# Four tiles of layer 0's output projection in the gaps of the last recurrent pair, tile 5 of their sum later, and the residual in the memory of keys and values

## The chip, the cores and the metric

The kernel runs on one core of one Trainium2 chip. The metric is the device time of one execution in microseconds (us), as the median of several runs; lower is better. TensorE multiplies matrices, VectorE and ScalarE do the elementwise work, GpSimd and SyncE mostly start transfers. Each engine has its own queue of instructions, in the order that the built program gives, and semaphores order the engines among each other. The profile calls TensorE PE (PEld for its weight loads), VectorE DVE, ScalarE ACT, GpSimd POOL and SyncE SP; SPq and POOLq are the queues of transfers that SP and POOL start.

## The reference

Two layers over 512 frames of width 1024, in float32. Layer 0 (mixer A) is a recurrent mixer of 12 heads of 64 beside a cross-attention of 4 heads into 256 memory tokens; layer 1 (mixer B) is a chunked attention. Both end the same way, and that end is what the change touches:

```python
mix, v_first = rwkv7_time_mix(h, p[..., :3 * D_MIX], ...)   # layer 0
q_mem = p[..., 3 * D_MIX:]
...
mo = memory_attention(q_mem, mem_n, w_mem_kv[layer])
x = x + jnp.concatenate([mix, mo], axis=-1) @ w_out[layer]
x = x + conv_glu(rms_norm(x, ln2[layer]), ffn_in[layer], ...)
```

The concatenation has 1024 columns: 768 of the recurrent heads and 256 of the memory heads. The residual x is added to the projection, and the sum, normed, feeds the gated feed-forward part.

## The kernel before

Activations lie transposed, the 1024 columns in 8 tiles of 128 partitions by 512 frames. Every float32 operand of the large products is split into a high and a low part (`r1h`, `r1l` for activations, `whi`, `wlo` for weights), and a product of a weight tile with an activation tile is three matmuls of 128x128 by 512: high by high (line 198), high by low (line 199), low by high (line 203). `dense` (line 190) writes one output tile: eight k tiles, so 24 matmuls, into one PSUM bank. `mm3` (line 183, matmuls at 184 to 186) is the same for one k tile. `load_w` (178) fetches 512 KB of weights into `wraw` (two buffers) and splits them into `whi`, `wlo` (three each); while `lo_on` is set, ACT writes the negated raw weights into `wlo` (172) and a POOL transfer adds the weights to them (173), else DVE subtracts (175).

The recurrent heads are worked on in six pairs. A pair has three parts: `prepare` (projections; writes the tiles `KB` and `v`, two buffers each), `front` (products inside the chunks of 64 frames; the last to read `KB` and `v`) and `back`. The end of `back` (lines 832 to 870) is a recursion over eight chunks: a small matmul (836), a DVE step (837), the next small matmul, and output matmuls (841) beside it; ACT then copies the result out (845), the heads are normed (`head_rsqrt`: matmuls at 550, a chain of small DVE steps, transposes at 559; then 857 to 859), multiplied by a gate (its product at 184 to 186, line 868), and split into `r1h[i]`, `r1l[i]` (215, 216). So pair 5, the last, gives tile 5, the last of the eight input tiles of the output projection. Memory attention for layer 0 (scores 922, transposes 287, values 297) gives tiles 6 and 7 (882, 883); tiles 0 to 3 come back from DRAM (888), and pair 4 gives tile 4.

`weave` takes generators, each with a cost and a list of what it has done, and emits instructions of the one that is least far in proportion to its cost. A generator may also wait for a condition. The scheduler of the tile framework then orders each engine's queue by readiness and priority. The last weave of layer 0 holds pair 4's `back`, pair 5's `front` and `back`, memory attention, and `ahead`: output tiles 0 and 1 over the seven k tiles other than 5, begun when memory attention and pair 5's recursion have been emitted. PSUM has eight banks: two D (`psd`), four S (`pss`), two L (`psl`). The L banks serve the recursion and the gate product of pairs 0 to 4, and pair 5's gate product; pair 5's recursion uses the D banks; `ahead` puts its two output tiles into the D banks.

After the weave the pools of the recurrent part are closed and `xT`, `r2h`, `r2l` are laid into the memory that comes free; four transfers load the residual into `xT` (line 955). `out_proj` then adds k tile 5 to output tiles 0 and 1, and computes tiles 2 to 7 whole. Each tile is added to `xT` (334), squared and summed (232, 234) and split into `r2h`, `r2l` (239, 240). The feed-forward part follows (its products go to the `psf` banks).

Of the kernel before, what the change touches and what calls it, by code (L numbers as in the profile page):

```python
# [10 lines left out]
F32 = mybir.dt.float32  # L11
# [7 lines left out]
P = 128  # L19
S = 512  # L20
KD = 8
# [60 lines left out]
def weave(gens, tc=None):  # L82

    live = [[g[0], float(g[1]), 0.0, 0.0, g[2] if len(g) > 2 else 0, None] for g in gens]
    now = 0.0
    while live:
        free = [e for e in live if e[5] is None or e[5]()]
        ready = [e for e in free if e[3] <= now]  # L90
        if not ready:
            now = min(e[3] for e in free)
            continue
        e = min(ready, key=lambda x: x[2] / x[1])
        e[5] = None
        try:
            with tc.high_priority(e[4]) if e[4] else ExitStack():
                y = next(e[0])
        except StopIteration:
            live.remove(e)  # L100
            continue
        if callable(y):
            e[5] = y
            continue
        cost, wait = y if isinstance(y, tuple) else (y, 0)
        now += cost
        e[2] += cost
        e[3] = now + wait
# [3 lines left out]
def trunk_kernel(ctx, tc, A, out):  # L112
# [211 lines left out]

    def out_proj(l, act, gain, h_, l_, xT, order, pre=(), done=()):
        for m in range(KD):
            if m < len(pre):
                w, ps = pre[m]
                run(dense(ps[:], [(w, K8)], act, order=[k for k in order if k not in done], start=False))
            else:  # L330
                w = load_w(A["w_out"][l, m])
                ps = ps_d()
                run(dense(ps[:], [(w, K8)], act, order=order))
# [41 lines left out]
    top, bot = slice(0, 64), slice(64, 128)  # L375
    HS = (top, bot)
    actx = ExitStack()
    open_banks(actx, S=4, L=2)
# [64 lines left out]
    def lora_split(idx, raw):  # L443
        w = split_w(raw[:], 1024)
        mraw = flat(kt_("KB", (P, NCH, 3, 64), bufs=2), 1)[:, 0, 0:1024]
        r3 = raw[:].rearrange("p (k f) -> p k f", k=8)
# [94 lines left out]
    def c3(ap):  # L541
        return ap.rearrange("p (c t) -> p c t", c=NCH)
# [23 lines left out]
    def prepare(i, T):  # L566
# [22 lines left out]
        def proj(j, nm, nxt):  # L589
# [7 lines left out]
            V.tensor_tensor(p_[:], ps[:], rho[:], op=ALU.mult)  # L597
            d = kt_("v", bufs=2) if nm == "v" else kt_("krv", bufs=2)
            SC.activation(d[:], p_[:], AF.Copy, scale=om[:, j * 6 + i:j * 6 + i + 1])
            V.scalar_tensor_tensor(d[:, 1:S], p_[:, 0:S - 1], Vc("mu_" + nm, i), d[:, 1:S], op0=ALU.mult, op1=ALU.add)  # L600
# [3 lines left out]
        Ei = kt_("Ei")  # L604
        KB = kt_("KB", (P, NCH, 3, 64), bufs=2)
        AR = kt_("AR", (P, NCH, 2, 64), bufs=2)
# [14 lines left out]
        def keys():  # L621
            k = T["k"]
            SC.activation(kn[:], k[:], AF.Copy, scale=kneg[:, i:i + 1])
            sq = tmp()
# [11 lines left out]
            SC.activation(f[:], th[:], AF.Identity, scale=kah[:, i:i + 1], bias=oka[:, i:i + 1])  # L636
            V.tensor_tensor(kh[:], k[:], f[:], op=ALU.mult)
            V.tensor_tensor(KB[:, :, 0, :], c3(kh[:]), c3(Ei[:]), op=ALU.mult)
# [39 lines left out]
        def bonus():  # L678
            r = T["r"]
            V.tensor_tensor(AR[:, :, 1, :], c3(r[:]), E[:, :, 1:65], op=ALU.mult)  # L680
            rk = tmp()
            V.scalar_tensor_tensor(rk[:], r[:], Vc("r_k", i), kh[:], op0=ALU.mult, op1=ALU.mult)
            rkh, rkl = tmp(F32R), tmp(F32R)
# [17 lines left out]
        yield next(bo)  # L701
        V.tensor_tensor(bon[:], T["pb"][:], T["v"][:], op=ALU.mult)
        T.update(KB=KB, AR=AR, dE=dE, bon=bon, Tt=Tt)
# [3 lines left out]
    def front(i, T):  # L707
        v, KB, AR, Tt = c3(T["v"][:]), T["KB"], T["AR"], T["Tt"]

# [58 lines left out]
    def back(i, T, dst, tiles=own_tiles, go=None):  # L768
# [84 lines left out]
        if go is not None:  # L853
            yield go
        pg = ps_l()
        mm3(pg[:], g2h[:], g2l[:], gsh[:], gsl[:], True, True)
# [59 lines left out]
    qmA = [kt_("kn")[:], kt_("kh")[:]]  # L916
    spare = flat(kt_("KB", (P, NCH, 3, 64), bufs=2), 3)
    ptA = [spare[:, 0], spare[:, 1], spare[:, 2], E[:].rearrange("p c t -> p (c t)")[:, :S]]
    prA = [kt_("a"), kt_("Ei")]
# [8 lines left out]
    def told(g, n):  # L928
        yield from g
        over.add(n)  # L930

    def ahead():
        yield lambda: "mem" in over and "state" in Ts[NPAIR - 1]
        yield from out_ahead(0, act1, AHEAD, 2, pre)

    def later(ns):
        yield 0, ns

    AHEAD = [0, 1, 2, 3, 4, 6, 7]
    a_, b_ = NPAIR - 2, NPAIR - 1  # L940
# [4 lines left out]
            16 * 648 + mem_cost(860)),  # L945
           (ahead(), 14 * 648)], tc)
    lo_on[0] = 0
    actx.close()

    mid = ctx.enter_context(tc.tile_pool(name="mid", bufs=1))  # L950
    xT = mid.tile([P, KD, S], F32, name="xT")
    r2h = mid.tile([P, KD, S], F32R, name="r2h")
    r2l = mid.tile([P, KD, S], F32R, name="r2l")
    for m in range(0, KD, 2):
        nc.sync.dma_start(xT[:, m:m + 2], A["xT"][:, m:m + 2])
    act2 = pair_of(r2h, r2l)
    fctx = ExitStack()
    open_banks(fctx, S=2, F=4)
    open_tmp(fctx, 6)
    out_proj(0, act1, "ln2_0", r2h, r2l, xT, AHEAD + [5], pre, AHEAD)  # L960
    norm_rho(acc, rho[:])
# [319 lines left out]
```

## Time and profile before

| | |
|---|---|
| median of 3 runs | 1376.41 us (1375.87 to 1377.62) |
| span of the profiled execution | 1375.2 us, from its first to its last instruction |
| mean granted TensorE clock | 0.989 of full |
| PE, PEld busy | 1320.1 us (96%), 1073.8 us (78%) |
| DVE, ACT, POOL busy | 827.1 us (60%), 612.6 us (45%), 34.0 us (2%) |
| first matmul of the feed-forward part of layer 0 (`psf`) | at 412.41 us |

The profiled execution's time outside its span isn't recorded with it: the three runs lie 0.7 to 2.4 us above the span, their median 1.2 us. Times in the views are us from the span's start. The view of windows gives the busy time of each engine in a stretch, the granted TensorE clock (1.00 is full speed) and the share of the transfer engines' time. In the chain of waits each row has a start, a duration, and an engine with the tile that it writes and the line; what released it stands in the row above.

### The profile page before, as it was taken

What the parts mean: (1) busy time and instruction counts of PE and PEld (TensorE: products, weight loads), DVE (VectorE), ACT (ScalarE), POOL (GpSimd) and SP (SyncE); (2) the same over time, 40 slices, a digit from 0 to 9 for tenths busy, and PEclk for the clock granted to TensorE, in tenths of its full rate; (3) what the DMA queues carried; (4) which work ended last, traced back from release to release, by engine and by line L of the source; (5) the groups of instructions that cost most, each with busy time, mean ns of one, the idle gap of its engine ahead of it and who ended that gap; (6) DMA issues with size and microseconds to landing.
All of it is one profiled execution on the core that took longest, in us unless ns stands there. A gap on an engine that the chain in (4) does not pass through costs nothing.

```text
span 1375.2 us, 20877 instructions
## 1 busy us (share of the span) xinstructions
PE 1320.1 (96%) x8266; PEld 1073.8 (78%) x8266; DVE 827.1 (60%) x1752; ACT 612.6 (45%) x1022; POOL 34.0 (2%) x55
## 2 busy tenths in 40 slices
PE   6989999999799999999999999999999999999996
PEld 4877777777588888888888878786788888888886
DVE  7876788878356655655333667657665565563324
ACT  6556565555234333333222566657443333332321
POOL 3000000000000000000000000000000000000000
PEclk9999999999899999999999999999999999999998
DMA  5366544462132233233232422222223223223332
GB/s 181 112 181 135 107 104 111 104 135 50 52 117 92 92 100 100 92 97 99 84 98 85 157 87 85 82 94 94 92 92 107 92 93 103 96 88 86 106 91 75
DMA packets 63507, 139.18 MB, mean 101 GB/s; under 512 B 24625, under 2 KB 28337, under 8 KB 63409
## 3 DMA queue, kind: packets, MB, share of 16 engines
q1 hardware_dynamic: 60672, 127.89, 29.8%
q0 software_dynamic: 2736, 9.96, 4.2%
q8 instruction: 65, 1.06, 0.3%
q14 instruction: 34, 0.27, 0.1%
HBM read 131.01 MB, written 6.82 MB: 100 GB/s over the span
## 4 chain that ended last, share of the span: by engine, by line
PE 78%; DVE 12%; ACT 4%; DMA 3%; issue 2%; SPq 0%; DVEq 0%; ACTq 0%; POOLq 0%
PE psf L198 12%; PE psf L199 12%; PE psf L203 12%; PE psd L198 10%; PE psd L199 10%; PE psd L203 10%; DVE Xu L667 2%; DVE Xs L669 1%; PE pss L1098 1%; DVE Xs L662 1%; DVE ML L720 1%; DVE wlo L175 1%; PE psd L1048 1%; PE pss L297 1%; ACT whi L169 1%
## 5 line engine op out<-in xcount | busy, mean ns | idle before, releaser
L175 DVE TENSOR_TENSOR wlo<-wraw,whi 128x1024 fp32r<-128x1024 f32 x183 | 219.0, 1197 | 132.3 <-PE psd L203 118.2
L169 ACT CAST whi<-wraw 128x1024 fp32r<-128x1024 f32 (+1 forms) x202 | 207.8, 1030 | 163.9 <-DMA wraw<-in_ffn_out_dram 41.5
L198 PE MATMUL psd<-r1h,whi 128*128 128x512 f32 x336 | 137.6, 410 | 7.5 <-ACT r1h L215 3.8
L198 PE MATMUL psf<-r2h,whi 128*128 128x512 f32 x352 | 137.1, 390 | 0.0
L198 PE MATMUL psf<-r1h,whi 128*128 128x512 f32 x352 | 137.1, 390 | 0.0
L199 PE MATMUL psf<-r1l,whi 128*128 128x512 f32 x352 | 136.9, 389 | 0.0
L199 PE MATMUL psf<-r2l,whi 128*128 128x512 f32 x352 | 136.9, 389 | 0.0
L199 PE MATMUL psd<-r1l,whi 128*128 128x512 f32 x336 | 134.9, 401 | 0.2 <-DVE r1l L216 0.2
L203 PE MATMUL psd<-r1h,wlo 128*128 128x512 f32 x336 | 91.3, 403 | 3.9 <-DMA wlo<-in_wA_dram 3.9
L199 PE MATMUL psd<-f3l,whi 128*128 128x512 f32 (+1 forms) x238 | 88.6, 377 | 0.0
L198 PE MATMUL psd<-f3h,whi 128*128 128x512 f32 (+1 forms) x238 | 88.5, 376 | 0.0
L359 DVE TENSOR_TENSOR tmp<-psf,rho 128x512 f32<-128x512 f32 x44 | 30.4, 692 | 94.7 <-PE psf L203 94.7
L203 PE MATMUL psf<-r1h,wlo 128*128 128x512 f32 x352 | 86.9, 389 | 0.0
L203 PE MATMUL psf<-r2h,wlo 128*128 128x512 f32 x352 | 86.9, 389 | 0.0
L198 PEld LDWEIGHTS psd<-r1h,whi 128*128 128x128 f32 x336 | 65.0, 193 | 23.7 <-ACT r1h L215 4.0
L198 PE MATMUL psd<-r2h,whi 128*128 128x512 f32 (+1 forms) x200 | 77.0, 389 | 0.8 <-ACT r2h L1105 0.7
L199 PE MATMUL psd<-r2l,whi 128*128 128x512 f32 (+1 forms) x200 | 76.4, 385 | 0.7 <-DVE r2l L216 0.7
L198 PEld LDWEIGHTS psf<-r2h,whi 128*128 128x128 f32 x352 | 66.1, 188 | 13.7
L199 PEld LDWEIGHTS psf<-r1l,whi 128*128 128x128 f32 x352 | 66.1, 188 | 13.7
L203 PEld LDWEIGHTS psf<-r1h,wlo 128*128 128x128 f32 x352 | 66.1, 188 | 13.7
L203 PEld LDWEIGHTS psf<-r2h,wlo 128*128 128x128 f32 x352 | 66.1, 188 | 13.7
L199 PEld LDWEIGHTS psf<-r2l,whi 128*128 128x128 f32 x352 | 66.1, 188 | 13.6
(352 smaller groups left out, 2420.9 us busy)
## 6 DMA issues: line engine op xcount, KB each, us to landing
wraw<-in_ffn_in_dram SPq DMA_DIRECT2D x88, 512.0 KB, 3.3
wraw<-in_ffn_out_dram SPq DMA_DIRECT2D x32, 448.0 KB, 3.3
wraw<-in_wA_dram SPq DMA_DIRECT2D x20, 512.0 KB, 3.9
wlo<-in_wA_dram POOLq DMA_DIRECT2D x17, 512.0 KB, 8.0
wraw<-in_w_out_dram SPq DMA_DIRECT2D x16, 512.0 KB, 3.4
wraw<-in_ffn_out_dram SPq DMA_DIRECT2D x16, 512.0 KB, 4.2
wraw<-in_wB_dram SPq DMA_DIRECT2D x8, 512.0 KB, 3.4
Lr<-d SPq DMA_DIRECT2D x24, 128.0 KB, 6.3
```

Source lines behind the costliest of these rows:

```text
L169: SC.copy(hi[:, :n], raw)
L175: V.tensor_tensor(lo[:, :n], raw, hi[:, :n], op=ALU.subtract)
L198: PE.matmul(ps, wh[:, j * P:(j + 1) * P], ah, start=start and n == 0, stop=False)
L199: PE.matmul(ps, wh[:, j * P:(j + 1) * P], al, start=False, stop=False)
L203: PE.matmul(ps, wl[:, j * P:(j + 1) * P], act(k)[0], start=False, stop=stop and n == len(ks) - 1)
L297: PE.matmul(pso[hs, :], vm[l][:, kt, (f * 2 + hh) * 64:(f * 2 + hh + 1) * 64], pts[f, hh, kt], start=kt == 0, stop=kt == 1)
L359: V.tensor_tensor(v[:], pv[:], rho[:], op=ALU.mult)
L662: V.scalar_tensor_tensor(X[:, m, q + 1:], L1[:, :, 0], X[:, m, q:q + 1], X[:, m, q + 1:], op0=ALU.mult, op1=ALU.add)
L667: V.tensor_tensor(uv, L1.rearrange("p i o -> p o i").to_broadcast([P, k, n]), X[:, 0:k, q:q + 1].to_broadcast([P, k, n]), op=ALU.mult)
L669: V.tensor_tensor(X[:, 0:k, q + 1:], X[:, 0:k, q + 1:], uv, op=ALU.add)
L720: V.tensor_tensor(ML[:, h, c4 * 4:c4 * 4 + 4, 0:128], ps[h][:], C("m1").unsqueeze(1).to_broadcast([P, 4, 128]), op=ALU.mult)
L1048: PE.matmul(pt, r1h[:, k, ts], wh[:, ws], start=k == 0, stop=False)
```

## The change

Layer 0 alone is touched. Six things are done together.

- `xT` gets memory of its own from the start, and the two buffers of `KB` and of `v` become parts of it (`KBs`, `vs`), as do three of the four tiles for memory attention's transposed weights (`ptA`) and the scratch of the low-rank weights. What is freed elsewhere equals what `xT` takes.
- `ahead` begins when memory attention and pair 4's `back` have been emitted, not when pair 5's recursion has; its first two tiles go to the L banks, two more follow in the D banks once the recursion is emitted. Pair 5's gate product moves from an L bank to an S bank for that.
- `ahead` has cost 0, and the new key of `weave` lets such a generator go on only when no other is ready.
- Its k order is 0, 1, 2, 3, 6, 7, 4, so that pair 4's tile comes last.
- The rows of the four weight tiles that belong to k tile 5 come in one transfer of 256 KB (line 951 of the changed kernel) and are split once, into the memory of `a` and `Ei`; so no weight tile is held for the end. When pair 5 is done, twelve matmuls (`mm3`) and four adds close output tiles 2, 3, 0, 1.
- The residual is loaded inside `ahead` (line 953 of the changed kernel), and `out_proj` only norms the first four tiles and computes tiles 4 to 7.

```diff
 def weave(gens, tc=None):
...
-        e = min(ready, key=lambda x: x[2] / x[1])
+        e = min(ready, key=lambda x: (x[1] <= 0, x[2] / (x[1] or 1.0)))
...
-    def out_proj(l, act, gain, h_, l_, xT, order, pre=(), done=()):
+    def out_proj(l, act, gain, h_, l_, xT, order, pre=(), done=(), added=0):
         for m in range(KD):
+            if m < added:
+                norm_tile(xT[:, m], m, gain, h_, l_)
+                continue
             if m < len(pre):
...
     HS = (top, bot)
+    mid = ctx.enter_context(tc.tile_pool(name="mid", bufs=1))
+    xT = mid.tile([P, KD, S], F32, name="xT")
+    KBs = [xT[:, 3 * u:3 * u + 3].rearrange("p m s -> p (m s)").rearrange("p (c a t) -> p c a t", c=NCH, a=3)
+           for u in range(2)]
+    vs = [xT[:, 6], xT[:, 7]]
...
-            d = kt_("v", bufs=2) if nm == "v" else kt_("krv", bufs=2)
+            d = vs[i % 2] if nm == "v" else kt_("krv", bufs=2)[:]
...
-        KB = kt_("KB", (P, NCH, 3, 64), bufs=2)
+        KB = KBs[i % 2]
...
-        pg = ps_l()
+        pg = ps_s() if i == NPAIR - 1 else ps_l()
...
-    spare = flat(kt_("KB", (P, NCH, 3, 64), bufs=2), 3)
-    ptA = [spare[:, 0], spare[:, 1], spare[:, 2], E[:].rearrange("p c t -> p (c t)")[:, :S]]
+    ptA = [xT[:, 0], xT[:, 1], xT[:, 2], E[:].rearrange("p c t -> p (c t)")[:, :S]]
...
+    AHEAD = [0, 1, 2, 3, 6, 7, 4]
+    NA = 4
+    w5 = {}
+
     def ahead():
-        yield lambda: "mem" in over and "state" in Ts[NPAIR - 1]
-        yield from out_ahead(0, act1, AHEAD, 2, pre)
+        yield lambda: "mem" in over and "back" in over
+        raw = tmp(F32, (P, NA, P))
+        for m in range(NA):
+            if m == 2:
+                yield lambda: "state" in Ts[NPAIR - 1]
+            w = load_w(A["w_out"][0, m])
+            if m == 0:
+                nc.sync.dma_start(raw[:], A["w_out"][0, 0:NA, :, 5 * P:6 * P].rearrange("m p f -> p m f"))
+                for u in range(0, KD, 2):
+                    nc.sync.dma_start(xT[:, u:u + 2], A["xT"][:, u:u + 2])
+            ps = (ps_l if m < 2 else ps_d)()
+            pre.append(ps)
+            yield from dense(ps[:], [(w, K8)], act1, order=AHEAD, stop=False)
+            if m == 0:
+                w5["h"], w5["l"] = (kt_(n_, (P, NA, P), dt=F32R) for n_ in ("a", "Ei"))
+                split_to(w5["h"][:], w5["l"][:], raw[:])
...
-    AHEAD = [0, 1, 2, 3, 4, 6, 7]
...
-           (ahead(), 14 * 648)], tc)
+           (ahead(), 0)], tc)
+    for m in (2, 3, 0, 1):
+        mm3(pre[m][:], w5["h"][:, m], w5["l"][:, m], r1h[:, 5], r1l[:, 5], False, True)
+        V.tensor_tensor(xT[:, m], xT[:, m], pre[m][:], op=ALU.add)
     lo_on[0] = 0
     actx.close()
 
-    mid = ctx.enter_context(tc.tile_pool(name="mid", bufs=1))
-    xT = mid.tile([P, KD, S], F32, name="xT")
+    mid = ctx.enter_context(tc.tile_pool(name="mid2", bufs=1))
     r2h = mid.tile([P, KD, S], F32R, name="r2h")
     r2l = mid.tile([P, KD, S], F32R, name="r2l")
-    for m in range(0, KD, 2):
-        nc.sync.dma_start(xT[:, m:m + 2], A["xT"][:, m:m + 2])
...
-    out_proj(0, act1, "ln2_0", r2h, r2l, xT, AHEAD + [5], pre, AHEAD)
+    out_proj(0, act1, "ln2_0", r2h, r2l, xT, AHEAD + [5], added=NA)
```

The remaining lines of the diff drop a `[:]` where a tile has become a view, and point the low-rank scratch at `xT`.

Lines in the changed kernel are 3 to 24 higher: 550, 559, 836, 841, 845, 882, 883 are now 558, 567, 844, 849, 853, 890, 891. On PE the two programs read alike, waits included, up to the gate product of pair 4. Three places differ in what the prediction speaks of.

On PE, the last two steps of pair 5's recursion, behind memory attention, before (`psd_4509` and `psd_4510` are the recursion's banks, `psd_4596` is output tile 0):

```order
L841 MATMUL psd_4510<-Lr_4352,AR_4351 64x64 x2
L836 MATMUL psd_4509<-AR_4351,Lr_4352 64x64 x2
L841 MATMUL psd_4510<-Lr_4352,AR_4351 64x64 x4
L198 MATMUL psd_4596<-r1h_68,whi_4591 128x512
L199 MATMUL psd_4596<-r1l_69,whi_4591 128x512
```

And now (`psd_4498` and `psd_4499` are the recursion's banks, `psl_4570` is output tile 0, `psl_4624` output tile 1):

```order
L198 MATMUL psl_4570<-r1h_68,whi_4560 128x512
L199 MATMUL psl_4570<-r1l_69,whi_4560 128x512
L203 MATMUL psl_4570<-r1h_68,wlo_4561 128x512 x4
L844 MATMUL psd_4498<-AR_4340,Lr_4341 64x64 x2
L849 MATMUL psd_4499<-Lr_4341,AR_4340 64x64 x2
L203 MATMUL psl_4570<-r1h_68,wlo_4561 128x512 x3
L849 MATMUL psd_4499<-Lr_4341,AR_4340 64x64 x2
L198 MATMUL psl_4624<-r1h_68,whi_4619 128x512
```

Six matmuls of output tile 0 stand before the recursion's last step and three before its last output matmuls; two and five more stand, in the same way, before the two steps ahead of these rows, and another five of tile 0 earlier, beside memory attention, where three matmuls of pair 5's gate product have moved away.

On PE, the end of the work ahead, before (`pss_4632` and `pss_4668` are the norm of pair 5's heads, `psd_4625` output tile 1, `psd_4729` output tile 2):

```order
L203 MATMUL psd_4625<-r1h_68,wlo_4621 128x512 x7
L559 MATMUL pss_4668<-cst_66,tmp_4666 128x128 x4
L198 MATMUL psd_4596<-r1h_68,whi_4591 128x512
L199 MATMUL psd_4596<-r1l_69,whi_4591 128x512
L203 MATMUL psd_4596<-r1h_68,wlo_4592 128x512
L198 MATMUL psd_4625<-r1h_68,whi_4620 128x512
L199 MATMUL psd_4625<-r1l_69,whi_4620 128x512
L203 MATMUL psd_4625<-r1h_68,wlo_4621 128x512
L198 MATMUL psd_4729<-r1h_68,whi_4725 128x512
```

And now (`psd_4718` is output tile 3; `a_4613` and `Ei_4614` hold the rows of k tile 5; `psd_4799` is output tile 4):

```order
L203 MATMUL psd_4718<-r1h_68,wlo_4714 128x512 x7
L184 MATMUL psd_4672<-r1h_68,a_4613 128x512
L185 MATMUL psd_4672<-r1l_69,a_4613 128x512
L186 MATMUL psd_4672<-r1h_68,Ei_4614 128x512
L184 MATMUL psd_4718<-r1h_68,a_4613 128x512
L185 MATMUL psd_4718<-r1l_69,a_4613 128x512
L186 MATMUL psd_4718<-r1h_68,Ei_4614 128x512
L184 MATMUL psl_4570<-r1h_68,a_4613 128x512
L185 MATMUL psl_4570<-r1l_69,a_4613 128x512
L186 MATMUL psl_4570<-r1h_68,Ei_4614 128x512
```

Where six matmuls of k tile 5 followed the norm directly, twelve now follow some thirty-six matmuls of output tiles 2 and 3, which stand behind the norm's transposes.

On ACT, around the end of memory attention, before (`E_91` is the last transposed weight tile, `psd_4510` the recursion's result):

```order
L290 COPY E_91<-pss_4550 128x512
L882 CAST r1h_68<-pss_4556 128x512
L845 COPY tmp_4585<-psd_4510 128x512
L848 ACTIVATE tmp_4587<-tmp_4585 128x512
L858 ACTIVATE tmp_4585<-tmp_4585,vec_67 128x512
L215 CAST r1h_68<-tmp_4585 128x512
L169 CAST whi_4762<-wraw_4760 128x1024
```

And now:

```order
L290 COPY xT_76<-pss_4528 128x512
L215 CAST a_4613<-tmp_4557 128x512
L290 COPY E_95<-pss_4539 128x512
L890 CAST r1h_68<-pss_4545 128x512
L169 CAST whi_4713<-wraw_4711 128x1024
L172 ACTIVATE wlo_4714<-wraw_4711 128x1024
L853 COPY tmp_4609<-psd_4499 128x512
L856 ACTIVATE tmp_4611<-tmp_4609 128x512
L169 CAST whi_4795<-wraw_4793 128x1024
```

The cast of k tile 5's rows (`a_4613`) stands ahead of the attention's last copy, and the two steps of output tile 3's weights (`whi_4713`, `wlo_4714`) stand ahead of the copy of the recursion's result.

More of the change, by code (lines that the diff above doesn't have):

```diff
@@ L444, in lora_split @@
         w = split_w(raw[:], 1024)
-        mraw = flat(kt_("KB", (P, NCH, 3, 64), bufs=2), 1)[:, 0, 0:1024]
+        mraw = xT[:, 3 * idx:3 * idx + 2].rearrange("p m s -> p (m s)")
         r3 = raw[:].rearrange("p (k f) -> p k f", k=8)
@@ L597, in proj @@
             V.tensor_tensor(p_[:], ps[:], rho[:], op=ALU.mult)
-            d = kt_("v", bufs=2) if nm == "v" else kt_("krv", bufs=2)
-            SC.activation(d[:], p_[:], AF.Copy, scale=om[:, j * 6 + i:j * 6 + i + 1])
+            d = vs[i % 2] if nm == "v" else kt_("krv", bufs=2)[:]
+            SC.activation(d, p_[:], AF.Copy, scale=om[:, j * 6 + i:j * 6 + i + 1])
             V.scalar_tensor_tensor(d[:, 1:S], p_[:, 0:S - 1], Vc("mu_" + nm, i), d[:, 1:S], op0=ALU.mult, op1=ALU.add)
@@ L622, in keys @@
             k = T["k"]
-            SC.activation(kn[:], k[:], AF.Copy, scale=kneg[:, i:i + 1])
+            SC.activation(kn[:], k, AF.Copy, scale=kneg[:, i:i + 1])
             sq = tmp()
@@ L636, in keys @@
             SC.activation(f[:], th[:], AF.Identity, scale=kah[:, i:i + 1], bias=oka[:, i:i + 1])
-            V.tensor_tensor(kh[:], k[:], f[:], op=ALU.mult)
+            V.tensor_tensor(kh[:], k, f[:], op=ALU.mult)
             V.tensor_tensor(KB[:, :, 0, :], c3(kh[:]), c3(Ei[:]), op=ALU.mult)
@@ L679, in bonus @@
             r = T["r"]
-            V.tensor_tensor(AR[:, :, 1, :], c3(r[:]), E[:, :, 1:65], op=ALU.mult)
+            V.tensor_tensor(AR[:, :, 1, :], c3(r), E[:, :, 1:65], op=ALU.mult)
             rk = tmp()
-            V.scalar_tensor_tensor(rk[:], r[:], Vc("r_k", i), kh[:], op0=ALU.mult, op1=ALU.mult)
+            V.scalar_tensor_tensor(rk[:], r, Vc("r_k", i), kh[:], op0=ALU.mult, op1=ALU.mult)
             rkh, rkl = tmp(F32R), tmp(F32R)
@@ L701, in prepare @@
         yield next(bo)
-        V.tensor_tensor(bon[:], T["pb"][:], T["v"][:], op=ALU.mult)
+        V.tensor_tensor(bon[:], T["pb"][:], T["v"], op=ALU.mult)
         T.update(KB=KB, AR=AR, dE=dE, bon=bon, Tt=Tt)
@@ L707, in front @@
     def front(i, T):
-        v, KB, AR, Tt = c3(T["v"][:]), T["KB"], T["AR"], T["Tt"]
+        v, KB, AR, Tt = c3(T["v"]), T["KB"], T["AR"], T["Tt"]
         ML = kt_("ML", (P, 2, NCH, 192), bufs=2)
```

## Prediction

> **What bounds the kernel now.** I read the page first.
>
> ```profile
> span 1375.2 us, 20877 instructions
> ...
> PE 1320.1 (96%) x8266; PEld 1073.8 (78%) x8266; DVE 827.1 (60%) x1752; ACT 612.6 (45%) x1022; POOL 34.0 (2%) x55
> ...
> PE   6989999999799999999999999999999999999996
> ...
> PEclk9999999999899999999999999999999999999998
> ```
>
> PE bounds the kernel. A slice is 34.4 us; the eleventh (344 to 378) has a 7 for PE and an 8 for the clock, and from the twelfth on PE reads 9 up to the last slice but one. So I take what is saved before 412 us, where the feed-forward part begins, as saved at the end: all that follows hangs on PE and moves with it. The changed stretch is the bad slice. The windows view, cut where the clock or the load changes, shows it:
>
> ```profile
> 351.60:355.00 3.40, 2.05 (x34) 1.45 (x31) 1.74 (x5) 0.61 (x2) 0.00 (x0) 1.00 0.00 0
> 355.10:358.40 3.30, 3.30 (x10) 2.52 (x9) 0.00 (x0) 0.87 (x2) 0.00 (x0) 0.50 0.00 0
> ...
> 367.50:371.20 3.70, 0.00 (x0) 0.00 (x0) 2.07 (x3) 1.43 (x2) 0.00 (x0) 1.00 0.00 0
> 372.20:376.80 4.60, 2.09 (x5) 1.07 (x4) 3.04 (x4) 2.09 (x2) 0.00 (x0) 0.50 0.83 289
> 376.90:382.40 5.50, 5.50 (x13) 4.34 (x14) 2.52 (x4) 2.36 (x4) 0.00 (x0) 0.50 0.89 329
> 382.60:412.40 29.80, 29.80 (x133) 24.65 (x132) 15.45 (x20) 12.55 (x16) 0.00 (x0) 1.00 0.27 89
> ```
>
> The first columns are the stretch, its length and PE's busy time; the third from the end is the granted clock. PE is part idle to 355, at half clock to 358.4, idle from 367.5 to 371.2, and half idle and then busy at half clock to 382.4. The chain of waits names the causes:
>
> ```profile
> 351.38 0.59 ACT r1h L882
> ...
> 353.66 0.36 PE psd L836 x4
> 354.04 0.29 DVE AR L837
> 354.38 0.33 PE psd L841 x4
> 354.71 0.43 PE psd L198
> ...
> 362.64 0.79 PE pss L550 x8
> ...
> 367.00 0.45 PE pss L559 x4
> ...
> 371.96 3.42 DMA xT<-in_xT_dram
> 375.46 0.67 issue
> 376.13 0.69 DVE xT L334
> 376.86 0.80 PE psd L198
> ...
> 405.15 1.81 PE psd L203 x8
> ...
> 410.59 1.81 PE psd L203 x8
> 412.41 0.23 PE psf L198
> ```
>
> To 354.71 the recursion's steps alternate between PE (836) and DVE (837); the norm of pair 5's heads (550, 559) ends in tile 5 at 371.96; then the residual's load, which could only start when the recurrent pools were free, holds the first add, and with it the bank of output tile 2, until 376.86. From there it is matmuls: an output tile takes 410.59 - 405.15 = 5.44 us, so one matmul 5.44 / 24 = 0.227 us at full clock.
>
> **The sum.** The projection has 8 x 24 = 192 matmuls, 43.5 us at full clock. With the norm's two groups (0.79 and 0.45) that is 44.8 us, and it takes 412.41 - 354.71 = 57.7. The 12.9 us over are the half clock and the two empty stretches. The matmuls stay the same in number (eight k tiles for eight tiles); what changes is where they stand.
>
> *Start of the recursion's last steps.* Five matmuls of output tile 0 are added beside memory attention and three of the gate product leave. The windows view shows no idle PE there:
>
> ```profile
> 333.36:344.00 10.64, 10.64 (x180) 9.04 (x181) 7.53 (x27) 7.56 (x23) 0.00 (x0) 1.00 0.01 4
> ```
>
> So two more cost 2 x 0.227 = 0.45 us; bounds 0 (all in small gaps that the busy time hides) and 5 x 0.227 = 1.1.
>
> *Recursion.* From the attention's last values (351.38, where ACT copies them out) to 354.71 are 3.3 us. They hold three steps of the recursion and its last output matmuls, four PE pieces of 0.33 to 0.36, 1.4 in all, so PE is idle for 1.9. Put in are 2 + 5 + 6 + 3 = 16 matmuls, 3.6 us: 1.9 fill the gaps, 1.7 push the recursion's end. Bounds 0 and 3.6. Its end moves to 354.71 + 0.45 + 1.7 = 356.9.
>
> *After it.* 192 - 21 = 171 matmuls are left, 38.8 us, plus 1.24 for the norm and 0.68 for the gate product: 40.7 us of PE work, if it never stops. I go through what it could stop for.
> - The norm's first group stands 12 matmuls (2.7 us) behind the recursion. It needs the copy and the square on ACT, which now queue behind the second step of tile 3's weights: that needs the buffer which tile 0's last matmul frees, 0.3 us before the recursion's end, and takes about 1.05 us (the cast of equal size below). With two more ACT steps of 0.6 the group is ready about 2.1 us after the recursion's end: covered by 0.6.
> - From the end of that group (363.43) to the transposes (367.00) are 3.57 us of small DVE steps. 15 matmuls, 3.4 us, stand between: 0.2 us lost.
> - From the transposes to the end of tile 5 are 371.96 - 367.00 = 5.0 us, plus up to 1.05 for a weight cast put ahead of the high part on ACT. Tiles 2 and 3 put 36 matmuls, 8.2 us, and the gate product in between: covered by 3 us. This is the 3.7 us empty stretch, gone.
> - The residual: two loads now go out before the pair's front has ended, two when the attention's values are read, near 352, and take 3.42; the first add is due near 374. The load that held 371.96 to 376.86 is gone with 19 us of cover.
> - Output tile 3's low weights are put on POOL's queue near 358. The view of transfers has, in its last column, the us from issue to landing:
>
> ```profile
> wraw<-in_w_out_dram SPq DMA_DIRECT2D x16, 512.0 KB, 3.4
> ...
> wlo<-in_w_out_dram POOLq DMA_DIRECT2D x2, 512.0 KB, 7.9
> ```
>
>   So they land near 366; they are first used 29 matmuls (6.6 us), the gate product and the transposes themselves behind the 364 of the row above, near 371.7.
> - The adds and norms of the first four tiles came one per output tile; now they come together beside tile 4. The groups of 376.8 to 412.4, with the mean ns of one behind the first bar:
>
> ```profile
> L169 ACT CAST whi<-wraw 128x1024 fp32r<-128x1024 f32 x6 | 6.3, 1052 | 12.7 <-issue 8.5 <-PE psd L199 4.1
> L175 DVE TENSOR_TENSOR wlo<-wraw,whi 128x1024 fp32r<-128x1024 f32 x5 | 6.1, 1220 | 0.0
> ...
> L334 DVE TENSOR_TENSOR xT<-xT,psd 128x512 f32<-128x512 f32 x7 | 4.7, 685 | 14.5 <-PE psd L203 14.5
> ```
>
>   Tile 4 needs only the first add's bank, which is closed three matmuls into the twelve: one split (1.22, whose buffer tile 3 frees) and one add (0.69) beside 12 matmuls of 2.7 us. Covered by 0.8. The weights of tiles 4 to 6 are split before that, those of tile 7 have over 10 us.
>
> SP's queue is reordered too: two residual loads and tile 4's weights stand ahead of the writes that carry pair 5's triangular inverse through DRAM. The timeline of SP, and of the engines that wait:
>
> ```profile
> 324.95 1.82 SPq L675 DMA_DIRECT2D Tt<-d  x4
> ...
> 329.07 0.43 SPq L772 DMA_DIRECT2D tmp<-in_g_dram  x1
> ```
>
> ```profile
> 330.42 0.89 DVE L776 STREAM_TRANSPOSE AR<-Tt 32x256 f32<-32x256 f32 x2
> ...
> 336.16 0.69 PE L781 MATMUL pss<-AR,ML 32*32 32x32 f32 x32
> ...
> 349.48 0.58 ACT L290 COPY E<-pss 128x512 f32<-128x512 f32 x1 [0.33 <-PE pss L287]
> ```
>
> The inverse (`Tt`) is taken up by DVE at 330.42 and its result by PE only at 336.16. Even if the queue or the shared transfer engines hold it by as much as a load of 512 KB takes (3.4), that stays inside the 5.7 us between the two. I take 0; bounds 0 and, if nothing hid it, 3.4.
>
> Sum: the feed-forward part starts at 356.9 + 40.7 + 0.2 = 397.8 in place of 412.41, 14.6 us sooner. Span 1375.2 - 14.6 = 1360.6; the median lay 1.2 above the span, so **1361.8 us**.
>
> The clock carries part of it: it read 0.50 in rows of 3.3, and of 4.6 and 5.5 us, and 1.00 elsewhere. The Trainium skill ("TensorE: Matmul & The Clock Gate", Part 1: The HAM clock gate) says the clock is halved after an idle window of about 3.4 us and given back after a busy one, the windows running free. In this case's rows the half clock from 355.10 followed a stretch in which PE was busy for 2.05 of 3.40 us, so a thin window was enough. By the Trainium skill's idle window the filled recursion stays warm and the time is 1361.8; the trace agrees with the length (3.3 us at 0.50), not with the idleness. By the row a window that is merely thin may cost the first rival below.
>
> **Rivals.**
> 1. *The clock still drops.* If the window over the recursion again counts as quiet, about 3.4 us after it run at half clock and do half the work: 1.7 us lost, 1363.5; twice, 1365.2. Against it: sixteen matmuls bring that stretch from 2.05 to nearly 3.4 busy. For it: the steps of the recursion are small matmuls, and a window's phase can shift. 14%.
> 2. *PE is fed too late.* The covers of 0.6 and 0.8 us are thin. If tile 4 waited for all four adds and a further split, 4 x 0.69 + 1.22 = 4.0 us, and the norm's first group for one more ACT step, about 1, it would be 5 us: 1366.8; half of it 1364.3. For: DVE and ACT do in one burst what was spread; against: they are half idle there (15.45 and 12.55 of 29.80). 10%.
> 3. *Slower: the transfer of k tile 5's rows stops two engines.* Its cast stands on ACT ahead of the attention's last copy, and its split on DVE between two steps of the recursion. It is the only transfer of its kind, in short pieces, and follows the 329.07 row on SP. Its turn on ACT comes where the last copy stood, 349.48, 20 us later. Every us beyond is lost whole, and slower than before begins at 349.5 + 14.6 = 364.1, 35 us after issue. The rows above give 3.4 to 7.9, so a landing after 40 us, 5 beyond that point, which gives 1376.4 + 5 = 1381, has 2%.
> 4. *It doesn't do what it says.* If keys, values and residual in one tile made pair i + 1 wait for pair i's reads, five stages would lose more than the gaps give, or all of it. But queues and waits read alike in both programs up to the gate product of pair 4. Then 1376; 2%.
>
> **Chances.** The forecast has 72%, rivals 14, 10, 2 and 2. Its own bounds: the recursion's push of 0 to 3.6 for 1.7, the start's of 0 to 1.1 for 0.45, put it between 1359.6 and 1364.3; the inverse's 3.4, which I hold for hidden, would reach 1365.2 from the forecast. The range reaches into the first two rivals, 1359.5 to 1366. A measurement of this kernel can tell about 0.2%, 2.8 us: faster by more 96%, within 2% (rival 4), slower 2% (rival 3).
>
> **What would show it.** After the change the first `psf` matmul stands near 398. The recursion's last output matmuls (line 849) end near 357, and matmuls to `psl` stand between its steps with no idle row for PE from 352 to 398 of over 0.5 us. The clock reads 1.00 in every window there. The adds at line 973 wait for PE and not for a transfer. Wrong would be: a clock row of 0.50 behind 355; a PE wait for the add of line 973 or for `wlo`; ACT waiting for `tmp<-in_w_out_dram` before 350; or a first 330 us that differ by more than 0.5 us.

## The result and the profile after

| | before | after |
|---|---|---|
| median of four runs each, on one chip | 1377.01 us (1375.87 to 1378.16) | 1368.09 us (1365.91 to 1371.56) |
| ratio | 1 | 0.9933 (95% interval 0.9913 to 0.9953) |
| median of all runs in the comparisons below | 1378.1 us (40 runs, 1374.3 to 1383.6) | 1366.9 us (17 runs, 1362.8 to 1371.6) |
| span of the profiled execution, granted clock | 1375.2 us, 0.989 | 1364.8 us, 0.993 |

The change is faster by 0.67% in the first comparison, 8.9 us; over all runs it is 11.1 us. The later comparisons ran on other chips, with medians of before from 1377.1 to 1379.8; in the two with six runs of the change it was 12.2 and 10.9 us faster. The forecast was 14.6 us less, 1361.8, with a range up to 1366.0: the sign and most of the mechanism held, the size did not.

The page of the changed kernel, the rows that answer to those of before:

```profile
span 1364.8 us, 20881 instructions
...
PE 1316.1 (96%) x8266; PEld 1070.6 (78%) x8266; DVE 825.4 (60%) x1751; ACT 615.1 (45%) x1025; POOL 35.5 (3%) x57
...
PE   6989999999999999999999999999999999999996
...
PEclk9999999999999999999999999999999999999998
```

The 7 and the 8 of the eleventh slice are gone. The windows view, cut at the gate product of pair 4, at the end of memory attention's values, at the recursion's end and at the first feed-forward matmul:

```profile
95.90:102.70 6.80, 5.52 (x24) 4.16 (x25) 2.41 (x9) 1.64 (x3) 0.86 (x1) 0.50 1.06 263
...
334.90:353.90 19.00, 18.69 (x293) 14.65 (x292) 11.08 (x34) 11.20 (x29) 0.00 (x0) 1.00 0.01 3
353.90:360.20 6.30, 6.30 (x54) 4.17 (x53) 1.83 (x5) 1.86 (x3) 0.00 (x0) 1.00 0.47 166
360.20:401.20 41.00, 41.00 (x186) 33.98 (x187) 24.73 (x42) 18.93 (x26) 0.86 (x1) 1.00 0.36 103
```

PE is busy throughout from 353.9 to 401.2, all of it at clock 1.00: none of the three holes of before is left. But the feed-forward part starts at 401.2, not at 397.8. Part of that is ahead of the change: the gate product of pair 4 stands at 334.9 in this execution and at 333.0 in the one before, although both programs are the same up to there, and the first row shows 6.8 us at half clock where before had 3.4. (A first 330 us that differ by more than 0.5 us was one of the prediction's signs of being wrong; experiment 1 looks into it.) The rest is the stretch from 353.9 to 360.2: 6.3 us, in place of 3.4. Here it is in the timeline of PE, row by row:

```profile
353.87 0.33 PE L844 MATMUL psd<-AR,Lr 64*64 64x64 f32 x4
354.04 0.28 PE L849 MATMUL psd<-Lr,AR 64*64 64x64 f32 x4
354.25 0.50 PE L199 MATMUL psl<-r1l,whi 128*128 128x512 f32 x1
354.59 0.40 PE L198 MATMUL psl<-r1h,whi 128*128 128x512 f32 x1
354.91 0.33 PE L844 MATMUL psd<-AR,Lr 64*64 64x64 f32 x4
355.08 0.28 PE L849 MATMUL psd<-Lr,AR 64*64 64x64 f32 x4
355.29 0.50 PE L199 MATMUL psl<-r1l,whi 128*128 128x512 f32 x1
355.63 0.39 PE L198 MATMUL psl<-r1h,whi 128*128 128x512 f32 x1
355.86 0.39 PE L199 MATMUL psl<-r1l,whi 128*128 128x512 f32 x1
...
356.63 0.33 PE L844 MATMUL psd<-AR,Lr 64*64 64x64 f32 x4
356.79 0.28 PE L849 MATMUL psd<-Lr,AR 64*64 64x64 f32 x4
357.00 0.50 PE L198 MATMUL psl<-r1h,whi 128*128 128x512 f32 x1
...
358.60 0.33 PE L844 MATMUL psd<-AR,Lr 64*64 64x64 f32 x4
358.76 0.28 PE L849 MATMUL psd<-Lr,AR 64*64 64x64 f32 x4
358.98 0.96 PE L203 MATMUL psl<-r1h,wlo 128*128 128x512 f32 x3
359.87 0.33 PE L849 MATMUL psd<-Lr,AR 64*64 64x64 f32 x4
```

Read the starts. Inside a group one projection matmul follows the other by 0.23 us (355.63, 355.86). The first of a group holds the next one off by 0.34 (354.25 to 354.59), and the last one holds the recursion's small matmul off by 0.32 (354.59 to 354.91): each switch there and back costs 0.20 us beside the matmuls. The four groups take 0.66, 1.34, 1.60 and 0.89 us, 4.49 in all, where 16 matmuls at 0.227 are 3.63. And the gaps that they fill, in the timeline of PE before, are these:

```profile
351.96 0.33 PE L836 MATMUL psd<-AR,Lr 64*64 64x64 f32 x4 [0.27 <-DVE AR L837]
...
352.94 0.33 PE L836 MATMUL psd<-AR,Lr 64*64 64x64 f32 x4 [0.53 <-DVE AR L837]
...
353.66 0.33 PE L836 MATMUL psd<-AR,Lr 64*64 64x64 f32 x4 [0.27 <-DVE AR L837]
...
354.38 0.33 PE L841 MATMUL psd<-Lr,AR 64*64 64x64 f32 x4 [0.27 <-DVE AR L837]
```

1.34 us, not 1.9. (The windows view of before says the same: 3.40 us with PE busy for 2.05 leave 1.35.) So most of what the 16 matmuls take is pushed onto the recursion's end. What was to be found out: is that the price of the groups, what are they worth then, and is the early 1.9 us the change's or the execution's?

### The profile page after: what moved, and what is told of

Same layout as the page of the kernel before. It is cut to its first block, busy times and chain, and to the rows that moved or that the text cites. A ratio compares the mean times of both kernels' runs of the same rounds, so it can differ in the third digit from the quotient of the medians.

```text
span 1364.8 us, 20881 instructions
## 1 busy us (share of the span) xinstructions
PE 1316.1 (96%) x8266; PEld 1070.6 (78%) x8266; DVE 825.4 (60%) x1751; ACT 615.1 (45%) x1025; POOL 35.5 (3%) x57
## 4 chain that ended last, share of the span: by engine, by line
PE 78%; DVE 12%; ACT 4%; DMA 3%; issue 2%; SPq 1%; DVEq 0%; ACTq 0%; POOLq 0%
PE psf L198 12%; PE psf L199 12%; PE psf L203 12%; PE psd L198 10%; PE psd L199 10%; PE psd L203 10%; DVE Xu L675 2%; DVE Xs L677 1%; PE pss L1122 1%; PE psl L203 1%; DVE Xs L670 1%; DVE ML L728 1%; PE pss L297 1%; PE psd L1072 1%; PE pss L1108 1%
## 5 line engine op out<-in xcount | busy, mean ns | idle before, releaser
L175 DVE TENSOR_TENSOR wlo<-wraw,whi 128x1024 fp32r<-128x1024 f32 (+1 forms) x181 | 216.5, 1196 | 132.5 <-PE psd L203 118.2
L198 PE MATMUL psd<-r1h,whi 128*128 128x512 f32 x318 | 127.4, 401 | 1.2 <-ACT whi L169 1.2
L199 PE MATMUL psd<-r1l,whi 128*128 128x512 f32 x318 | 124.9, 393 | 0.0
L203 PE MATMUL psd<-r1h,wlo 128*128 128x512 f32 x318 | 86.7, 405 | 4.4 <-DMA wlo<-in_wA_dram 4.4
L198 PEld LDWEIGHTS psf<-r2h,whi 128*128 128x128 f32 x352 | 66.1, 188 | 13.6
L198 PEld LDWEIGHTS psf<-r1h,whi 128*128 128x128 f32 x352 | 66.1, 188 | 13.6
```

Of the source, the lines that this page charges most:

```text
L175: V.tensor_tensor(lo[:, :n], raw, hi[:, :n], op=ALU.subtract)
L198: PE.matmul(ps, wh[:, j * P:(j + 1) * P], ah, start=start and n == 0, stop=False)
L199: PE.matmul(ps, wh[:, j * P:(j + 1) * P], al, start=False, stop=False)
L203: PE.matmul(ps, wl[:, j * P:(j + 1) * P], act(k)[0], start=False, stop=stop and n == len(ks) - 1)
```

## Experiments

The table holds one profiled execution a row, read at the same four places, in us; half clock is the length of the 0.50 rows. "Pushed" is from the end of memory attention's values to the recursion's end.

| kernel | gate product at | half clock between 90 us and it | gate product to first psf | pushed | recursion's end to psf | half clock in there |
|---|---|---|---|---|---|---|
| before | 333.0 | 3.4 | 79.2 | 3.4 | 57.5 | 3.4 + 10.2 |
| before, again | 332.7 | 3.4 | 78.8 | 3.5 | 57.0 | 3.4 + 10.2 |
| change | 334.9 | 6.8 | 66.3 | 6.3 | 41.0 | none |
| change, second | 334.7 | 6.8 | 66.3 | 6.3 | 41.0 | none |
| change, third | 336.4 | 3.4 + 6.8 | 68.9 | 6.3 | 41.0 | 6.8, at 340.6 |
| change, fourth | 331.2 | 3.4 | 66.3 | 6.3 | 41.0 | none |
| empty recursion | 331.9 | 3.4 | 70.3 | 3.4 | 49.0 | 6.8, at 353.8 |
| residual alone | 333.3 | 6.8 | 74.5 | 3.4 | 52.8 | 3.4 + 3.4 |
| fewer in gaps | 334.3 | 6.8 | 66.7 | 4.9 | 42.8 | none |
| projection rated | 336.9 | 3.4 + 3.4 + 3.4 | 72.1 | - | 38.2 | 6.8, at 340.8; 3.4, at 371.5 |
| two tiles | 334.6 | 6.8 | 66.5 | 5.8 | 40.9 | none |

**1. Is the early shift the change's?** The changed kernel, unedited, three more times, and the kernel before once more. The first:

> The changed kernel once more, nothing edited. Theory: its program is the same as before up to 318 us, and the 1.9 us by which its profile was late at the gate product (334.98 for 333.02) are one more half-clock window and slower transfers of that one execution. Then this profile has the gate product anywhere from 332.5 to 335.5, the half-clock windows ahead of 330 us differ in number or place between the profiles, and the spans of the timed runs follow the lost clock: 1.37 us for each 0.001 of granted clock. Rival: the shared memory makes the first 330 us slower; then the gate product stands at 334.5 or later again with the same windows. Time 1365.5 to 1371.5 either way, 8 to 9 us below before.

Measured: 1366.05 us (six runs, 1362.79 to 1369.25), ratio 0.9908 (0.9888 to 0.9928); the gate product at 334.7, again with 6.8 us of half clock near 96. This alone did not tell the two apart. The kernel before:

> The kernel before once more, nothing edited, for a second profile of it. Theory: the gate product of pair 4 moves by up to 2 us from 333.02, with the windows of half clock ahead of it; the windows behind 350 us come back (355 and 372 to 382), since the empty stretches there are part of the program. Rival: 333.0 within 0.3, and the shift of 1.9 us then belongs to the change. Time 1376 to 1378.5.

Measured: 1376.29 us, the gate product at 332.7, 3.4 us of half clock near 98; the windows over the recursion and behind the norm came back at their places (353.9 and 371.0). The change a third time:

> The changed kernel a third time, for its clock windows and the gate product's place. Theory: the gate product lies between 331.9 and 335 according to whether the half-clock window near 96 to 102 lasted 3.4 or 6.8 us; from the gate product to the first feed-forward matmul 66.3 us whatever happened ahead. Rival (the change itself delays the first 330 us): 334.8 again with a window of 3.4.

Measured: 1370.47 us, and the gate product later still, with three half-clock rows behind 90 us where there had been one:

```profile
98.20:101.60 3.40, 3.40 (x20) 2.45 (x19) 0.00 (x0) 0.00 (x0) 0.00 (x0) 0.51 1.05 261
169.90:176.70 6.80, 6.80 (x73) 5.25 (x73) 4.06 (x8) 3.22 (x6) 0.00 (x0) 0.50 0.15 48
340.60:347.40 6.80, 6.80 (x80) 5.39 (x78) 2.79 (x14) 3.27 (x12) 0.00 (x0) 0.50 0.01 2
```

The third of them lies inside the stretch counted on: it costs 2.6 us there (68.9 for 66.3). The forecast of 66.3 whatever happened ahead was wrong by that. The fourth time:

> The changed kernel a fourth time, beside the two-tile version, for more times and one more profile. Theory: median 1366 to 1370, 9 to 12 us below before; from the gate product to the first feed-forward matmul 66.3 us, or 1.7 us more for each 3.4 us of half clock inside it; the gate product at 333 or 334.8 or 336.4 according to the half-clock windows near 96 and 170. Rival (the early shift belongs to the change): never below 334.5.

Measured: 1366.18 us (six runs), ratio 0.9922 (0.9900 to 0.9945). In its profiled execution:

```profile
96.70:100.10 3.40, 3.40 (x21) 2.43 (x19) 0.00 (x0) 0.23 (x1) 0.00 (x0) 0.50 1.05 279
331.20:350.30 19.10, 18.79 (x294) 14.73 (x295) 11.08 (x34) 11.22 (x30) 0.00 (x0) 1.00 0.02 5
350.30:356.50 6.20, 6.20 (x53) 4.05 (x53) 1.83 (x5) 1.82 (x3) 0.00 (x0) 1.00 0.50 166
356.50:397.50 41.00, 41.00 (x188) 34.00 (x187) 24.72 (x42) 18.96 (x26) 0.86 (x1) 1.00 0.34 103
```

The gate product stands at 331.2, ahead of both profiles of before. The rival that the change delays the first 330 us falls. Taking off half of the half clock ahead of it, the gate product lies at 331.3 and 331.0 before, and at 331.5, 331.3, 331.3 and 329.5 in the change; the last is the only one of the six with no half clock near 23 us either, where the others had 3.4 or 6.8. So the shift goes with the execution's own clock windows and not with the program. Whether the change makes such windows more frequent, two profiles of before can't tell; the granted clocks of the timed runs (mean 0.992 in 17 runs of the change, 0.988 in 36 of before) give no sign of it: their difference is worth some 11.5 us of half clock, and the rows that went behind the recursion had 13.6. The windows also go with part of the spread of the timed runs: the change's two fastest (1362.8 and 1362.9) were granted 0.995 and 0.996 of the clock, its slowest three (1369.6, 1370.5 and 1371.6) 0.991, 0.989 and 0.989. Another part does not show in the granted clock, and its cause is open: at 0.989 runs of before took from 1374.6 to 1380.1. A comparison of one execution with one can therefore be off by several us here.

**2. What are the matmuls between the recursion's steps worth?** They were taken out:

```diff
             if m == 0:
...
+                w1 = load_w(A["w_out"][0, 1])
+                yield lambda: "state" in Ts[NPAIR - 1]
             ps = (ps_l if m < 2 else ps_d)()
             pre.append(ps)
+            if m < 2:
+                SC.copy(ps[:, 0:2], Ts[NPAIR - 1]["yc"][:, 0:2])
```

The copy writes two columns of the bank from the recursion's output, so that its first matmul can't come sooner. The weights of tile 1 and the split of k tile 5's rows are asked for ahead of it. The five matmuls of tile 0 beside memory attention move behind the recursion too.

> The change, but its first two output tiles start only when the recursion's output has been copied, so that no projection matmul stands between the recursion's steps. Theory now: a group of projection matmuls between two steps costs some 0.2 us beside its matmuls (the first row after a switch stands 0.33 before the next one, not 0.23), so the 16 matmuls in four groups hid only 0.8 us; the stretch from the attention's last values to the recursion's end goes back from 6.3 to 3.5 us, the matmuls stand behind it, and the time is 0.8 us above the change with the clock at 1.00, or 2.5 us above it where the thin stretch halves the clock for one window of 3.4 us. The forecast's own account (1.9 us of gaps filled): 1.9 us above the change, 3.6 with the window. Rival, that the groups cost more than the gaps give: at or below the change.

Measured: 1370.52 us (ratio 0.9944, 0.9924 to 0.9965), 4.5 above the change on the same chip. Its windows over the recursion and behind it:

```profile
349.90:353.30 3.40, 2.09 (x38) 1.48 (x37) 1.73 (x5) 0.59 (x1) 0.00 (x0) 1.00 0.85 292
353.80:360.60 6.80, 6.80 (x20) 5.57 (x19) 0.00 (x0) 0.89 (x4) 0.00 (x0) 0.50 0.00 1
360.60:402.20 41.60, 41.60 (x187) 34.39 (x186) 24.72 (x42) 19.10 (x25) 0.86 (x1) 1.00 0.34 102
```

The recursion is back at 3.4 us, PE 2.09 of 3.40 busy, and 6.8 us of half clock follow. From the gate product to psf it takes 70.3 for 66.3: 4.0, of which 6.8 / 2 = 3.4 are the clock (PE is busy for all 6.8) and the remaining 0.6 what all 21 matmuls had hidden. The price of 0.8 for gaps alone held roughly; one window was expected and two came. The forecast's 1.9 us of filled gaps would have given 1.9 + 3.4 = 5.3. The rival that groups cost more than they give fell.

**3. Does every further matmul in there cost its full time?**

```diff
+                yield lambda: "state" in Ts[NPAIR - 1]
             ps = (ps_l if m < 2 else ps_d)()
```

The rest is as in experiment 2. Without its copy the scheduler still puts ten matmuls into the gaps.

> The change with the first tile's matmuls asked for only behind the recursion, so that they take second place: 10 matmuls instead of 16 stand between its steps, in groups of 2, 4, 2 and 2. Theory (0.2 us a group beside its matmuls, 1.34 us of gaps): from the attention's last values to the recursion's end 3.4 + 10 x 0.227 + 4 x 0.2 - 1.34 = 5.1 us, where the change took 6.3; the six matmuls stand behind it, the clock stays at 1.00, and the time is that of the change within 1 us. Rival (no cost of a switch): 4.3 us, and the time 0 to 1 us below the change. Rival (the clock needs all sixteen): a half-clock row over the recursion and 1.7 to 3.4 us above the change.

Measured: pushed 4.9 us, nearer the 5.1 of the theory than the 4.3 without a cost of switching; 1368.68 us (ratio 0.9922, 0.9897 to 0.9948), as the change. From ten to sixteen matmuls the push grows by 1.4 us, 0.23 for each: with four groups of these sizes the gaps are full, and no more is hidden. The two-tile version of experiment 6 lies between, with 14 matmuls and 5.8 us.

```profile
353.30:358.20 4.90, 4.90 (x48) 3.02 (x47) 1.83 (x5) 1.04 (x2) 0.00 (x0) 1.00 0.62 214
358.20:401.00 42.80, 42.55 (x194) 35.04 (x193) 24.77 (x42) 19.76 (x27) 0.86 (x1) 1.00 0.33 99
```

Ten matmuls also kept the clock at 1.00, in the one profile taken.

**4. Must the projection be confined to gaps?**

```diff
-           (ahead(), 0)], tc)
+           (ahead(), 28 * 648)], tc)
```

> The change with one number: the projection's share in the weave is its own cost and no longer 0, so that it isn't confined to gaps. Tiles 0 and 1 then stand whole ahead of the recursion's last three steps. Theory: those steps run through an empty PE again (1.1 us of gaps, and one or two half-clock windows, 1.7 or 3.4 us), and only tiles 2 and 3, 9.5 us of matmuls, are left to cover the 12 to 17 us from the recursion's end to tile 5, so 2 to 6 us more are lost: 5 to 10 us above the change. Rival: the order among the steps does not matter as long as PE has work; within 1 us of the change.

Measured: 1369.92 us, ratio 0.9924 (0.9893 to 0.9954): 1.2 us above the version of experiment 3 on the same chip. The theory's 5 to 10 us fell. In its profile psf comes 72.1 us after the gate product. The 6.8 us of half clock at 340 cost 3.4 of that by half their length, or 2.6 as in the change's third profile, which leaves 68.7 to 69.5, 2.4 to 3.2 above the change: one window of half clock (1.7) and 0.7 to 1.5 for gaps. Its windows over the recursion's last steps:

```profile
366.00:371.40 5.40, 3.67 (x38) 2.57 (x37) 1.99 (x4) 1.52 (x2) 0.00 (x0) 1.00 0.88 225
371.50:374.90 3.40, 3.40 (x10) 2.61 (x9) 0.00 (x0) 0.65 (x2) 0.00 (x0) 0.50 0.05 16
```

The lack of cover that the theory feared did not come: tile 5's first product stands at 384.39, 13.5 us behind the recursion's end (370.9), and PE waits for next to nothing.

**5. Which part is the residual's?** The shared memory and the early load alone, with the order, the cost and the two tiles of before:

```diff
     def ahead():
         yield lambda: "mem" in over and "state" in Ts[NPAIR - 1]
+        for u in range(0, KD, 2):
+            nc.sync.dma_start(xT[:, u:u + 2], A["xT"][:, u:u + 2])
         yield from out_ahead(0, act1, AHEAD, 2, pre)
```

> The memory part alone: keys, values and residual share one tile and the residual is loaded early, but two tiles ahead with all seven k tiles as before, their matmuls behind the recursion and tile 5 as before. Theory: the load of 3.4 us and the bank held by it go (2.5 us of empty PE between 372.2 and 376.8), and with them one or two of the three half-clock windows from 372 to 382 (1.7 to 3.4 us); the empty stretch from 367.5 to 371.2 stays. 4.2 to 5.9 us faster than before, about 1372. Rival: the load was hidden behind the norm anyway and something else holds the first add: within 1 us of before. Second rival: the shared tile costs the first 330 us about 2 us: 2 to 4 us faster, with the gate product at 335.

Measured: 1371.94 us (twelve runs), ratio 0.9965 (0.9949 to 0.9982), so 2.5 to 7.0 us below before, where 4.2 to 5.9 were expected. Its profile was of an execution 9.5 us above that median (psf 76.7 us after the gate product, with 10.2 us of half clock at 343 and 3.4 at 381 between them), so it was profiled again:

> The memory part alone a second time, for a profile: the first was of an execution 8 us above its own median, with half-clock windows at 172 and 343 that no other had. Theory: the first residual add no longer waits for a transfer; PE is still part empty from the norm's second group to tile 5; half clock in one window over the recursion and one or two behind 370; first feed-forward matmul 5 to 7 us earlier against the gate product than in the kernel before (72 to 74 us for 79). Rival: the half clock behind 370 is as long as before (10.2 us) and the gain is the load's 2.5 us alone.

```profile
351.60:355.00 3.40, 2.06 (x37) 1.44 (x38) 1.74 (x5) 0.59 (x1) 0.00 (x0) 1.00 0.86 282
355.20:358.60 3.40, 3.40 (x9) 2.63 (x8) 0.00 (x0) 1.02 (x2) 0.00 (x0) 0.50 0.04 16
...
367.50:372.10 4.60, 0.70 (x3) 0.19 (x1) 2.69 (x4) 1.43 (x2) 0.00 (x0) 1.00 0.00 0
372.20:375.60 3.40, 3.38 (x8) 2.67 (x9) 2.12 (x3) 2.44 (x4) 0.00 (x0) 0.51 0.02 5
```

74.5 us from the gate product to psf, 4.5 less than the mean of before (79.0) and just short of the 72 to 74 expected. In the timeline of PE before, the load is the idle time in the second row:

```profile
371.23 0.50 PE L198 MATMUL psd<-r1h,whi 128*128 128x512 f32 x1 [3.79 <-ACT r1h L215]
...
376.86 0.80 PE L198 MATMUL psd<-r1h,whi 128*128 128x512 f32 x1 [2.57 <-DVE xT L334]
```

These 2.57 us are gone, as expected. The half clock behind 372 lasts 3.4 in place of 10.2, but before PE had worked for only 2.09 + 5.50 = 7.6 of those 10.2 us, so what went is worth an estimated (7.6 - 3.4) / 2 = 2.1, not half of 6.8. The two make 4.7 of the 4.5 measured. The empty stretch between the norm's transposes and tile 5 (the 3.79 of the first row) stays, as expected.

**6. Are four tiles needed?**

```diff
-    NA = 4
+    NA = 2
...
-    for m in (2, 3, 0, 1):
+    for m in range(NA):
```

> The change with two output tiles ahead instead of four (both with k tile 5 later; tiles 2 and 3 follow in the ordinary loop, eight k tiles each). Theory: in the change tile 5's high part is ready 11.9 us after the recursion's end and first used 16.5 us after it, so 4.6 us of cover were spare; here 37 matmuls, both norm groups and the gate product, 10.3 us, stand before its first use, so PE is empty for 1.6 us, with a half-clock window (1.7 us) if that counts as idle: 1.6 to 3.3 us above the change from the gate product to the first feed-forward matmul (68 to 69.7 for 66.3). Rival: four tiles are what closes the stretch; with two it opens again as in the memory part alone (74.5 us, 8 above the change). Rival: no difference, 66.3.

Measured: 66.5 us from the gate product to psf; 1369.35 us, ratio 0.9937 (0.9913 to 0.9961), beside 1366.18 and 0.9922 (0.9900 to 0.9945) for the change on the same chip, intervals that overlap. The last rival held: no difference that these runs can tell, and the expected 1.6 us of empty PE did not come. ACT and PE of the two-tile version say why:

```profile
370.33 0.62 ACT L215 CAST r1h<-tmp 128x512 fp32r<-128x512 f32 x1 [1.55 <-DVE tmp L876]
```

```profile
371.10 0.65 PE L184 MATMUL psl<-r1h,a 128*128 128x512 f32 x2
```

The cast that makes tile 5's high part ends at 370.95, 10.7 us behind the recursion's end (360.24) and just ahead of its use. In the change a weight cast for a later output tile stands ahead of it on ACT:

```profile
370.51 1.05 ACT L169 CAST whi<-wraw 128x1024 fp32r<-128x1024 f32 x1 [1.00 <-PE psd L199]
371.47 0.62 ACT L215 CAST r1h<-tmp 128x512 fp32r<-128x512 f32 x1
```

With fewer tiles ahead that cast comes later. None of the versions beat the change by more than the runs can tell.

## Why the prediction was off

**What held.** All three holes went, and for the reasons given. By the table and the rows of before, the 12.7 us from the gate product to psf (79.0 to 66.3) are: the empty stretch between the transposes and tile 5, 4.0 (3.79 and 0.23 behind it; the residual alone and the empty recursion, 74.5 and 70.3, differ by 4.2); the wait for the load, 2.6; half clock, 5.5, half of the 11.0 us that PE worked at it; what the matmuls in the gaps hid, 0.6. From the recursion's end to psf 40.9 us were forecast and 41.0 measured in all four profiles. The covers held (the norm's groups, the residual, tile 4's bank, `wlo`); tile 5's cover of 3 us was 4.6. The adds (line 973) followed DVE's split of tile 4's weights, which ends at 378.1, and waited for no transfer; the rows of k tile 5 stopped nobody. None of the four rivals came: the clock did not drop over the filled recursion. In the fourth profile psf even stands at 397.6, where the forecast has 397.8, but that is luck: that execution reached the gate product 1.8 us earlier than before did.

**The step that failed** is the one named *Recursion*: "1.9 fill the gaps, 1.7 push the recursion's end". The push was 6.26 - 3.40 = 2.86. Two things were wrong in it. The idle time was got by taking four PE pieces off 3.3 us, when the timeline shows gaps of 1.34 (1.6 by the difference 4.49 - 2.86), and so does the prediction's own row for 351.60 to 355.00, with PE busy for 2.05 of 3.40. And a matmul was priced at 0.227 wherever it stands, though in the timeline of before the first matmul after the recursion's small ones already holds the next off by 0.33 (354.64 to 354.97); four groups cost 4.49 - 3.63 = 0.86 that no term held. The *start* was 0.75 (19.0 us from the gate product to the last values, for 18.3), forecast 0.45: there too the five matmuls came in pieces between small ones.

**What the sum left out.** Behind psf the change takes some 0.7 us longer (963.4 to 964.1, for 962.9 and 963.0), in two places of about 0.4 each. One is a wait of PE for ACT: 0.81 and 0.90 in the profiles of before (the first row below is one), 1.26, 1.49, 1.15 and 1.05 in those of the change (the second row). It was 0.63 in the two-tile version; why it varies is open.

```profile
790.90 0.38 PE L1048 MATMUL psd<-whi,r1h 128*128 128x256 f32 x1 [0.81 <-ACT vS L1052]
```

```profile
780.12 0.39 PE L1072 MATMUL psd<-whi,r1h 128*128 128x256 f32 x1 [1.26 <-ACT vS L1076]
```

The other stands behind PE's last matmul: from its end to the end of the span it is 7.1 us in both profiles of before and 7.5 in all four of the change. There SP goes through a row of semaphore instructions, some 0.06 us apart. From the end of its last long wait for the output's transfers on, it has three of them left before and ten now:

```profile
L1276 SPq EVENT_SEMAPHORE  x3: 17/17/28, 1374.3 to 1375.1; - x3
...
L1300 SPq EVENT_SEMAPHORE  x10: 17/28/28, 1363.5 to 1364.7; - x10
```

It is 7.1 with the residual alone too, and 7.5 in experiments 2, 3, 4 and 6.

The base was wrong too, by 0.6 to 1.7 us: "the median lay 1.2 above the span" compared one execution with three others. Every execution with both numbers has 1.7 to 1.9 (1366.57 and 1364.8), and the median of before is 1377.0 in the four runs of the first comparison and 1378.1 over all runs, not 1376.4. From 1378.1, 14.6 less would be 1363.5. Of the 3.4 us that the change's 1366.9 lies above it, 1.2 are the recursion, 0.3 the start, 0.1 the stretch after it, 0.7 behind psf, and some 0.6 the half clock at 340 (2.6 us in one of four profiles). The remaining 0.5 is less than the runs scatter.

**The clock.** The forecast kept it at 1.00 over a filled recursion and left a dropped one 14%. In the change's four profiles and in experiments 3 and 6 the recursion was filled and no half clock followed it; where it was empty, half clock followed in both profiles of before and in experiments 2, 4 and 5, the disturbed first profile of experiment 5 excepted. The Trainium skill ("TensorE: Matmul & The Clock Gate", Part 1: The HAM clock gate) says that the window runs freely, and that the number of cold matmuls at a kernel's start varies from run to run with it. The runs show the like far behind the start: the half clock comes in lengths of 3.4, 6.8 and 10.2 us, and one program had it at 96, at 170 and at 340 or not. The forecast reckoned with the half clock in the stretch it changed and not in the 330 us ahead of it, where the rows of the table are worth 1.7 to 5 us of each execution.

## What to carry to other kernels

A gap of 0.3 us between the steps of a serial chain is hardly worth filling for its own time: each group of large matmuls put there costs 0.2 us of switching, so four groups returned 0.6 us; what paid was that PE stayed busy enough to keep its clock, 3.4 us, and ten matmuls did that as well as sixteen. Read gaps from the idle times in the timeline, not from a stretch less some pieces, and price a matmul by where it stands. Count a half-clock row by what PE does in it, not by its length: where PE waits anyway it costs nothing. Before a few us are argued about, profile both kernels twice and take off the half clock ahead of the change.

## What the runs showed of the hardware

Half clock does not need an idle PE in the records. In the third profile of the change the clock halved at 340.6 after this window:

```profile
337.10:340.50 3.40, 3.40 (x53) 2.84 (x53) 2.52 (x9) 0.95 (x4) 0.00 (x0) 1.00 0.01 2
```

PE counts as busy for all of it, but with small matmuls, as the groups of that window show:

```profile
L929 PE MATMUL pss<-kmT,kh 64*128 64x256 f32 x8 | 2.0, 389 | 0.0
L558 PE MATMUL pss<-cst,tmp 128*128 128x2 f32 x8 | 0.9, 240 | 0.0
L789 PE MATMUL pss<-AR,ML 32*32 32x32 f32 x32 | 0.7, 192 | 0.0
```

The same instructions ran at 1.00 in the other three profiles of the change, so small matmuls are not enough by themselves; that the phase of the window decides is only argued. A stretch of small matmuls is to be counted as a place where the clock may drop.
